# A hybrid convolution and attention block on one core: attention's copies, low parts and sums on separate products, two leading columns moved off GpSimd, attention steps placed anew

## The chip, the core and the metric

The kernel runs on one core of a Trainium2 chip. Its engines work side by side, each through its own queue in program order, and wait for one another by semaphores: TensorE (PE in the profile; PEld is its loading of weights), VectorE (DVE), ScalarE (ACT), GpSimd (POOL) and SyncE (SP). SP issues transfers only; POOL issues some of them between its own instructions. The metric is device time in microseconds (us). Before the change three runs took 2007.78, 2001.44 and 2006.52 us; their median is 2006.52 us.

## The reference, cut to what matters

One layer over 2048 positions of 1024 features, float32 throughout:

```python
h = rms_norm(x, norm_g)
v_c, b_c, c_c, z_c, q, k, v, z_a, gate_logits = jnp.split(jnp.einsum('bsd,dc->bsc', h, w_in), ...)
y_c = b_c * causal_depthwise_conv(c_c * v_c, conv_w)          # width 3: positions s-2, s-1, s
y_a = jnp.einsum('bsc,cd->bsd', y_c * silu(z_c), w_conv_out)
q = rms_norm(q per head, q_norm_g); k = rms_norm(k per head, k_norm_g)
o = sliding_window_attention(q, k, v, sinks) * silu(z_a)      # 16 heads of 64, 4 kv heads, window 128
y_b = jnp.einsum('bsc,cd->bsd', o, w_attn_out)
g_a, g_b = jnp.split(jax.nn.sigmoid(gate_logits + gate_b), 2, axis=-1)
x = x + jnp.einsum('bsd,de->bse', g_a * y_a + g_b * y_b, w_out)
```

Attention works on blocks of 128 positions, each against its own block and the one before it, with one learned sink per head in the softmax's sum.

## The kernel before, in words

**Tiles and units.** The sequence is done in two tiles of 1024 positions (t = 0, 1), and each tile in two halves of 512. A float32 operand is split into a high and a low part, and a matrix product is the sum of three (high by high, high by low, low by high). Every projection is cut into **units** of one weight group (`sunit`, from L424). A unit has seven products in the manner of Strassen's method, each of 12 matmuls of 128x512 (L412, in `product`), issued in the order 1, 5, 6, 2, 7, 3, 4. They land in three banks of PSUM: `X` takes products 1 and 2, `V` takes 5 and 3, `Y` takes 6, 7 and 4. Between them the side engines do the sums. After product 1 ACT copies `X` into `Y` (L430). After 5 ACT copies `V` into a spare tile `s5` (L439). After 6 DVE adds `V = s5 + Y`; product 7 writes `Y`, so this sum has the length of one product (2) to be done in. After 7 DVE adds `Y + s5`. The finished four quarters go to the unit's own closing function (`fin`).

**Weights.** A unit's weights are loaded as float32, and their sums and splits are made by pieces, one piece per product and some units ahead: a high part on ACT (L308, tiles ending in `_ah`, `_sh`, `_th`, `_d`), a low part on DVE (`_al`, `_sl`, `_tl`). DVE's instructions all carry L213, the line of the helper that records them.

**The order of the work.** It is written out by hand. `run` (from L599) counts one **tick** per product: it emits the product with its closing sums, then the weights' high part, then the first function that was put on this tick, then the weights' low part, then the other functions of the tick. Emission order is each engine's queue order. A function is put on a tick by `put(n, f)`.

**Stages of a tile** (times of tile 0 and tile 1 are in the table below): keys, values and queries; then the convolution, four times the unit sequence cv, cv, b (21 ticks); then the gates ga and gb (8 units each 7 ticks); then za and z (the SiLU gates), the two output projections ya and yb (L1143), and after both tiles the last projection o.

**Attention** runs beside the convolution and the gates: 32 steps a tile, each for a head group j and a block b. A step is placed on a tick n, and its parts on ticks counted from n by constants (L57): its loads at n-5 and n+V_ (SP); scores at n (PE L923 and L927, then a mask, a maximum and four short instructions on DVE); exponentials at n+1 (ACT L949 and four of L952); division at n+2 (DVE, three instructions); the flip at n+F_ (a DVE transposition into `f`, then a POOL-issued transfer to memory, `fd<-f`, L972); the way back at n+B_ (four POOL-issued transfers `x<-fd`, L979); the turn at n+X_ (ACT `xh` L986 and `yp` L987, DVE's low part `xl = x - xh`, four masks on POOL at L996); the product with the values at n+O_ (PE L1013, into `po`); and the output at n+O_+1, which for each of two halves copies one part of `po` by ACT (L1024) and adds the other by DVE, then stores.

**The convolution's closing function** (`fin_cv`, from L1030) gathers u = c*v, with two leading columns ahead of it, and one tick after the last product calls `edge`: GpSimd fills the leading columns (L1048 in tile 0, zeros; L1050 in tile 1, from a small tile `halo`), in tile 0 it keeps the last two columns in `halo` (L1052), and ACT then makes the first tap of both halves (L1055). The two other taps follow on DVE, one half on each of the two next ticks.

Of the kernel before, what the change touches and what calls it, by code (L numbers as in the profile page):

```python
# [19 lines left out]
H = 512  # L20
# [33 lines left out]
PE_TURNS = ((0, 0), (0, 1))  # L54
TURN_WAIT = 3

V_, F_, B_, X_, O_ = 6, 2, 5, 9, 13  # L57
HALVES = (LH, UH)


# [1 line left out]
def block_kernel(  # L62
# [12 lines left out]
    nc = tc.nc  # L75
# [18 lines left out]
    def slot(shape, dt, name):  # L94
        return big.tile(shape, dt, tag="big", name=name)
# [123 lines left out]
    vec = Woven()  # L219
# [383 lines left out]
    def run(gen):  # L603
        while True:
            tick[0] += 1
            if next(gen, gen) is gen:
                tick[0] -= 1
                return
            ahead_loads()
            hi, lo = (piece() if tick[0] >= W_FROM else None) or (None, None)  # L610
            if hi:
                hi()

            fs = at.pop(tick[0], [])
            for f in fs[:1]:
                f()
            if lo:
                lo()
            for f in fs[1:]:
                f()  # L620
            vec.some(WOVEN)

# [359 lines left out]
    def att_turn(t, j, b, pt):  # L982
        nm = f"{t}_{j}_{b}"
        xh, xl = slot([P, G, P], F32R, f"xh{nm}"), slot([P, G, P], F32R, f"xl{nm}")
        y = slot([P, G, P], F32R, f"yp{nm}")
        nc.scalar.copy(xh, pt)  # L986
        nc.scalar.copy(y[LH], pt[UH])  # L987
        vec.tensor_tensor(out=xl, in0=pt, in1=xh.bitcast(F32), op=ALU.subtract)

        def keep(dst, src, prev):
            sg = 1 if prev else -1
            d4 = dst.rearrange("p (e s) (g q) -> p e s g q", s=2, q=32)
            s4 = src.rearrange("p (e s) (g q) -> p e s g q", s=2, q=32)
            nc.gpsimd.affine_select(  # L996
                out=d4, in_=s4, pattern=[[0, 2], [-32 * sg, 2], [0, G], [-sg, 32]],
                compare_op=ALU.is_gt if prev else ALU.is_ge, fill=0.0, base=0,
                channel_multiplier=sg)

        keep(xh[UH], xh[UH], False)
        keep(y[LH], y[LH], True)
        keep(y[UH], xl[UH], True)
        keep(xl[UH], xl[UH], False)
        return xh, xl, y
# [12 lines left out]
    def att_out(t, j, b, po):  # L1018
        pov = po.rearrange("p (h e s c q) -> p h e s c q", h=2, e=2, s=2, c=2)
        o = slot([P, 2, P], F32, f"o{t}_{j}_{b}")  # L1020
        for e in range(2):
            own, oth = HALVES[e], HALVES[1 - e]
            ov = o[own].rearrange("p c (h s q) -> p h s c q", h=2, s=2)
            nc.scalar.copy(ov, pov[oth, :, e])  # L1024
            add(ov, pov[own, :, e], ov)
        nc.sync.dma_start(
            od[t][2 * j : 2 * j + 2, :, b * P : (b + 1) * P].rearrange("c p q -> p c q"), o)


    def fin_cv(t, k, ys):  # L1030
        u = upool.tile([P, 2 * H + 2], F32, tag="u", name=f"u{t}_{k}")
        halves = [u[:, 2 : 2 + H], u[:, 2 + H :]]
        hold = {}

        def fin(i, q, val):
            if (i, q) == (0, 0):
                nc.scalar.copy(halves[0], val)
            elif (i, q) == (1, 1):
                hold["v"] = plain(val, f"vr{t}_{k}")
            elif (i, q) == (0, 1):  # L1040
                mul(halves[1], val, hold["v"])
            else:
                mul(halves[0], val, halves[0])
                put(tick[0] + 1, edge)

        def edge():
            if t == 0:
                nc.gpsimd.memset(u[:, 0:2], 0.0)  # L1048
            else:
                nc.gpsimd.tensor_copy(u[:, 0:2], halo[:, k, :])  # L1050
            if t + 1 < NT:
                nc.gpsimd.tensor_copy(halo[:, k, :], u[:, 2 * H :])  # L1052
            for h in range(2):
                y = ys[k, h] = slot([P, H], F32, f"y{t}_{k}_{h}")
                nc.scalar.activation(out=y, in_=u[:, h * H : h * H + H], func=AF.Copy, scale=tap(0, k))  # L1055
            put(tick[0] + 1, lambda: taps(0))
            put(tick[0] + 2, lambda: taps(1))

        def taps(h):
            y = ys[k, h]  # L1060
            for i in (1, 2):
                vec.scalar_tensor_tensor(
                    out=y, in0=u[:, h * H + i : h * H + i + H], scalar=tap(i, k), in1=y,
                    op0=ALU.mult, op1=ALU.add)

        return fin
# [411 lines left out]
    def attention(t, places):  # L1478
        for r, n in enumerate(places):
# [13 lines left out]
            put(n + F_, step("f", lambda g, j=j, b=b: att_flip(t, j, b, g["n"])))  # L1493
            put(n + B_, step("b", lambda g, j=j, b=b: att_back(t, j, b, g["f"])))
            put(n + X_, step("x", lambda g, j=j, b=b: att_turn(t, j, b, g["b"])))
            put(n + O_, step("o", lambda g, j=j, b=b: att_values(t, j, b, g["x"], g["v"])))
            put(n + O_ + 1, step("z", lambda g, j=j, b=b: att_out(t, j, b, g["o"])))

    def next_tile(t, n0):

# [53 lines left out]
    for t in range(NT):  # L1554
# [3 lines left out]
        if t == 0:  # L1558
            t0 += 1

        attention(t, [t0 + 48 + 21 * (r // 4) + (0, 6, 10, 15)[r % 4] for r in range(16)] + [
            t0 + 129 + int(3.75 * r) for r in range(16)])
        if t > 0:
            run(sunit(("k", t), ops, fin_k(t)))
            run(sunit(("v", t), ops, fin_v(t)))
# [111 lines left out]
```

## Time and profile before

The profiled execution took 2005.35 us, of which the profile's span is 2003.6 us. Stages by their stretch of the span:

| stage | stretch, us | length, us | PE busy, us |
|---|---|---|---|
| keys, values, queries, tile 0 | 0 to 150 | 150 | 140.79 |
| convolution, tile 0, with attention | 150 to 400 | 250 | 246.59 |
| gates, tile 0, with attention | 400 to 600 | 200 | 192.62 |
| za, z, ya, yb of tile 0; k, v, q of tile 1 | 600 to 1045 | 445 | 443.99 |
| convolution, tile 1, with attention | 1045 to 1320 | 275 | 257.06 |
| gates and first za units, tile 1, with attention | 1320 to 1566 | 246 | 238.13 |
| the rest | 1566 to 2003.6 | 437.6 | 433.03 |

A row of the windows by stage reads: stretch and length, then for PE, PEld, DVE, ACT and POOL the busy time with the number of instructions, then the clock granted to TensorE (1.00 is full), the share of the transfer engines and GB/s. A row of the timeline reads: start, duration, engine, line, operation, what it writes and reads, and in brackets how long the engine had been idle before it and which instruction ended that. A row of the waits reads: the waiting instruction, what released it, then the total in us, how often, and the longest. A row of the groups by form reads: line, engine, operation, tiles, shape and count, then busy time in us and the mean of one in ns, then idle time ahead of the group and what ended it.

### The profile page before, as it was taken

What the parts mean: (1) busy time and instruction counts of PE and PEld (TensorE: products, weight loads), DVE (VectorE), ACT (ScalarE), POOL (GpSimd) and SP (SyncE); (2) the same over time, 40 slices, a digit from 0 to 9 for tenths busy, and PEclk for the clock granted to TensorE, in tenths of its full rate; (3) what the DMA queues carried; (4) which work ended last, traced back from release to release, by engine and by line L of the source; (5) the groups of instructions that cost most, each with busy time, mean ns of one, the idle gap of its engine ahead of it and who ended that gap; (6) DMA issues with size and microseconds to landing.
All of it is one profiled execution on the core that took longest, in us unless ns stands there. A gap on an engine that the chain in (4) does not pass through costs nothing.

```text
span 2003.6 us, 27366 instructions
## 1 busy us (share of the span) xinstructions
PE 1952.2 (97%) x8846; PEld 1607.5 (80%) x8846; DVE 1447.8 (72%) x2492; ACT 931.7 (47%) x1862; POOL 556.3 (28%) x850
## 2 busy tenths in 40 slices
PE   9999999999999999999999998899999999999999
PEld 7778877877788888888878787778878788888887
DVE  7989888887876564388798778778777556356654
ACT  7655455555664342235465444456565434222321
POOL 1472344354452000200562332335445000100000
PEclk9999999999999999999999999999999999999999
DMA  8485555566776435863674544567777434865553
GB/s 297 108 225 156 160 159 160 169 212 193 220 229 216 163 106 178 315 232 116 186 186 149 163 141 138 143 173 227 219 235 224 157 122 154 264 202 173 163 173 110
DMA packets 217374, 366.53 MB, mean 183 GB/s; under 512 B 29264, under 2 KB 104016, under 8 KB 217232
## 3 DMA queue, kind: packets, MB, share of 16 engines
q1 hardware_dynamic: 189696, 288.96, 45.8%
q0 software_dynamic: 27392, 75.80, 13.4%
q8 instruction: 70, 1.15, 0.2%
q14 instruction: 72, 0.59, 0.1%
q10 hardware_dynamic: 144, 0.03, 0.0%
HBM read 251.17 MB, written 113.51 MB: 182 GB/s over the span
## 4 chain that ended last, share of the span: by engine, by line
PE 53%; DVE 21%; DMA 8%; issue 6%; ACT 6%; POOL 3%; SPq 1%; DVEq 0%; POOLq 0%; ACTq 0%
PE Y L412 16%; PE yb L1143 9%; PE ya L1143 8%; DVE st L213 2%; PE Vo L412 2%; PE Xo L412 2%; PE Xz L412 2%; PE Vza L412 2%; PE Vz L412 2%; ACT p L952 2%; PE Xza L412 2%; DVE y L213 2%; DVE wcv_raw L213 1%; DMA x<-fd 1%; PE Xga L412 1%
## 5 line engine op out<-in xcount | busy, mean ns | idle before, releaser
L979 POOL DMA_DIRECT2D x<-fd x256 | 140.1, 554 | 47.7 <-DMA fd<-f 23.6
L996 POOL TENSOR_SCALAR_AFFINE_SELECT xh<-xh 64x512 fp32r<-64x512 f32 x64 | 63.0, 985 | 261.2 <-DVE xl L213 169.3
L952 ACT ACTIVATE p<-s,st,rq 128x128 f32<-128x128 f32 x256 | 112.8, 450 | 0.2 <-DMA lows<-kd 0.2
L972 POOL DMA_DIRECT2D fd<-f x64 | 37.0, 578 | 252.0 <-DVE f L213 181.1
L213 DVE TENSOR_TENSOR o<-po,o 64x256 f32<-64x256 f32 x128 | 53.2, 415 | 57.7 <-ACT o L1024 57.4
L213 DVE SCALAR_TENSOR_TENSOR tha<-tha,ya 128x512 f32<-128x512 f32 x32 | 22.0, 688 | 96.1 <-PE ya L1143 93.3
L1024 ACT COPY o<-po 64x256 f32<-64x256 f32 x128 | 46.9, 367 | 83.2 <-DVE o L213 81.1
L1143 PE MATMUL ya<-opa,wya_1h 128*128 128x512 f32 x256 | 79.5, 391 | 0.9 <-ACT opa L240 0.5
L412 PE MATMUL Xcv<-oph,wcv_ah 128*128 128x512 f32 x256 | 79.4, 391 | 0.0
L1143 PE MATMUL yb<-opb,wyb_1h 128*128 128x512 f32 x256 | 78.9, 389 | 0.0
L1143 PE MATMUL yb<-opb,wyb_0h 128*128 128x512 f32 x256 | 78.9, 389 | 0.0
L1143 PE MATMUL ya<-opa,wya_0h 128*128 128x512 f32 x256 | 78.8, 389 | 0.0
L240 ACT CAST opb<-ocr 128x512 fp32r<-128x512 f32 x32 | 19.9, 621 | 112.8 <-DMA ocr<-ocd 111.3
L213 DVE TENSOR_TENSOR xl<-x,xh 128x512 fp32r<-128x512 f32 x64 | 43.9, 687 | 35.4 <-ACT xh L986 30.0
L213 DVE SCALAR_TENSOR_TENSOR y<-u,cols,y 128x512 f32<-128x512 f32 x64 | 51.6, 807 | 20.1 <-ACT y L1055 17.4
L1231 POOL DMA_DIRECT2D wo<-in_w_out x16 | 8.7, 543 | 194.1 <-DVE opb L213 179.8
L521 POOL DMA_DIRECT2D x<-in_x x8 | 4.3, 540 | 201.4 <-PE ya L1143 200.6
L412 PE MATMUL Y<-oph,wcv_th 128*128 128x512 f32 x128 | 45.5, 440 | 13.2 <-DVE Vcv L213 13.2
L1143 PEld LDWEIGHTS ya<-opa,wya_1h 128*128 128x128 f32 x256 | 48.0, 188 | 12.2 <-ACT opa L240 1.3
L1143 PEld LDWEIGHTS ya<-opa,wya_0h 128*128 128x128 f32 x256 | 48.0, 188 | 10.0
L1143 PEld LDWEIGHTS yb<-opb,wyb_0h 128*128 128x128 f32 x256 | 48.0, 188 | 9.9
L1143 PEld LDWEIGHTS yb<-opb,wyb_1h 128*128 128x128 f32 x256 | 48.0, 188 | 9.9
(591 smaller groups left out, 6379.5 us busy)
## 6 DMA issues: line engine op xcount, KB each, us to landing
wcv_raw<-in_w_in SPq DMA_DIRECT2D x32, 512.0 KB, 4.1
q<-q2d SPq DMA_DIRECT2D x64, 256.0 KB, 4.7
fd<-f POOLq DMA_DIRECT2D x64, 256.0 KB, 4.0
x<-fd POOLq DMA_DIRECT2D x256, 64.0 KB, 3.8
v<-vd SPq DMA_DIRECT2D x128, 128.0 KB, 4.1
gd<-th SPq DMA_DIRECT2D x64, 256.0 KB, 2.8
wq_raw<-in_w_in SPq DMA_DIRECT2D x16, 512.0 KB, 5.2
q2d<-q_h POOLq DMA_DIRECT2D x64, 128.0 KB, 4.8
```

Source lines behind the costliest of these rows:

```text
L213: r = f(*args, **kw)
L240: nc.scalar.copy(hi, src)
L412: nc.tensor.matmul(ps, lhsT=w[:, j, :], rhs=b[:, m, :], start=start and j == 0 and i == 0, stop=j == KP - 1 and i == 2, skip_group_check=n ...
L521: eng.dma_start(xt, x2[r0 : r0 + P, :])
L952: nc.scalar.activation(out=p[:, i, :], in_=sg[:, i, HD : 3 * HD], func=AF.Exp, bias=st[:, 1, i : i + 1], scale=rv[:, i // 2, i % 2 : i % 2 ...
L972: nc.gpsimd.dma_start(fd, f)
L979: nc.gpsimd.dma_start(x[QUADS[k]], src[k])
L996: nc.gpsimd.affine_select(out=d4, in_=s4, pattern=[[0, 2], [-32 * sg, 2], [0, G], [-sg, 32]], compare_op=ALU.is_gt if prev else ALU.is_ge, ...
L1024: nc.scalar.copy(ov, pov[oth, :, e])
L1143: nc.tensor.matmul(ps, lhsT=w[:, j, cs], rhs=o[:, m, :], start=n == 0 and i == 0, stop=n == KC - 1 and i == 2)
L1231: nc.gpsimd.dma_start(h, w_o[c * P : (c + 1) * P, hs(q)])
```

## The change

Five edits.

1. The constants of an attention step: its value load moves from n+6 to n+4, the way back from n+5 to n+4; the flip, the turn and the product with the values keep theirs (2, 9, 13).
2. The turn at n+9 keeps only ACT's two copies; the low part on DVE and the four masks on POOL become a function of their own at n+10.
3. The output at n+14 keeps only ACT's two copies; the two sums on DVE and the store come at n+15.
4. The leading columns: zeros by DVE, the copies from and to `halo` by ACT.
5. The steps' ticks: the first 16 of a tile go three ticks later; of the second 16 the first goes three ticks later and the spacing is 3.5 instead of 3.75. And in `run` up to three functions of a tick, not one, are emitted ahead of the weights' low part.

```diff
-V_, F_, B_, X_, O_ = 6, 2, 5, 9, 13
+V_, F_, B_, X_, L_, O_, S_ = 4, 2, 4, 9, 10, 13, 15
...
             fs = at.pop(tick[0], [])
-            for f in fs[:1]:
+            for f in fs[:3]:
                 f()
             if lo:
                 lo()
-            for f in fs[1:]:
+            for f in fs[3:]:
                 f()
...
         nc.scalar.copy(xh, pt)
         nc.scalar.copy(y[LH], pt[UH])
+        return pt, xh, xl, y
+
+    def att_low(got):
+        pt, xh, xl, y = got
         vec.tensor_tensor(out=xl, in0=pt, in1=xh.bitcast(F32), op=ALU.subtract)
...
+        parts = []
         for e in range(2):
...
             nc.scalar.copy(ov, pov[oth, :, e])
-            add(ov, pov[own, :, e], ov)
+            parts.append((ov, pov[own, :, e]))
+        return o, parts
+
+    def att_sum(t, j, b, got):
+        o, parts = got
+        for ov, pv in parts:
+            add(ov, pv, ov)
         nc.sync.dma_start(
...
             if t == 0:
-                nc.gpsimd.memset(u[:, 0:2], 0.0)
+                vec.memset(u[:, 0:2], 0.0)
             else:
-                nc.gpsimd.tensor_copy(u[:, 0:2], halo[:, k, :])
+                nc.scalar.copy(u[:, 0:2], halo[:, k, :])
             if t + 1 < NT:
-                nc.gpsimd.tensor_copy(halo[:, k, :], u[:, 2 * H :])
+                nc.scalar.copy(halo[:, k, :], u[:, 2 * H :])
...
             put(n + X_, step("x", lambda g, j=j, b=b: att_turn(t, j, b, g["b"])))
-            put(n + O_, step("o", lambda g, j=j, b=b: att_values(t, j, b, g["x"], g["v"])))
+            put(n + L_, step("w", lambda g: att_low(g["x"])))
+            put(n + O_, step("o", lambda g, j=j, b=b: att_values(t, j, b, g["w"], g["v"])))
             put(n + O_ + 1, step("z", lambda g, j=j, b=b: att_out(t, j, b, g["o"])))
+            put(n + S_, step("t", lambda g, j=j, b=b: att_sum(t, j, b, g["z"])))
...
-        attention(t, [t0 + 48 + 21 * (r // 4) + (0, 6, 10, 15)[r % 4] for r in range(16)] + [
-            t0 + 129 + int(3.75 * r) for r in range(16)])
+        attention(t, [t0 + 51 + 21 * (r // 4) + (0, 6, 10, 15)[r % 4] for r in range(16)] + [
+            t0 + 132 + int(3.5 * r) for r in range(16)])
```

DVE's queue has 2494 instructions before and 2502 after, ACT's 1593 and 1607, POOL's 855 and 831; PE's 8848 and SP's 1266 stay.

What this does to the queues is shown at three places, all in the convolution of tile 1, about the unit of weights `wcv_3`, whose profiled products before lie near 1140 us. A name such as `o_0_2` is head group 0, block 2, with a buffer number behind it; `s_0_4` are the scores of step 4. The next unit's weights, `wb_1`, are being made in the third.

DVE, before, the last rows up to the unit's sum `Vcv_3` (the mask and maximum of `s_0_4` stand some rows further up):

```order
L213 TENSOR_TENSOR st_0_4_10733<-st_0_4_10733 128x4
L213 RECIPROCAL st_0_4_10733<-st_0_4_10733 128x4
L213 TENSOR_TENSOR p_0_4_10755<-p_0_4_10755,st_0_4_10733 128x512
L213 STREAM_TRANSPOSE f_0_4_10798<-p_0_4_10755 128x512
L213 TENSOR_TENSOR o_0_2_10822<-po_0_2_10788,o_0_2_10822 64x4x2x32 x2
L213 TENSOR_TENSOR xl_0_3_10829<-x_0_3_10697,xh_0_3_10828 128x512
L213 SCALAR_TENSOR_TENSOR y_2_0_10803<-u_2_10568,cols,y_2_0_10803 128x512 x2
L213 TENSOR_TENSOR Vcv_3_10807<-s5cv_3_10820,Y 128x512
```

and DVE of the change at the same sum:

```order
L213 TENSOR_TENSOR xl_0_2_10718<-x_0_2_10574,xh_0_2_10717 128x512
L213 TENSOR_TENSOR o_0_1_10750<-po_0_1_10710,o_0_1_10750 64x4x2x32 x2
L213 COPY_PREDICATED s_0_4_10781<-mask_i,s_0_4_10781 128x4x64
L213 TENSOR_REDUCE st_0_4_10789<-s_0_4_10781 128x4
L213 TENSOR_TENSOR st_0_4_10789<-st_0_4_10789,rq_0_9609 128x4
L213 SCALAR_TENSOR_TENSOR st_0_4_10789<-st_0_4_10789,nsink_r 128x4
L213 TENSOR_TENSOR st_0_4_10789<-cols,st_0_4_10789 128x4
L213 SCALAR_TENSOR_TENSOR y_2_0_10759<-u_2_10527,cols,y_2_0_10759 128x512 x2
L213 TENSOR_TENSOR Vcv_3_10763<-s5cv_3_10776,Y 128x512
```

Step 4's division and flip, which stood ahead of `Vcv_3`, now follow it; its mask and maximum have come down to just ahead of it. The output sums and the low part ahead of it are those of steps 1 and 2, where they were of steps 2 and 3.

ACT, before, at the same products:

```order
L430 COPY Y<-Xcv_3_10770 128x512
L1055 ACTIVATE y_2_0_10803<-u_2_10568,cols 128x512
L1055 ACTIVATE y_2_1_10805<-u_2_10568,cols 128x512
L439 COPY s5cv_3_10820<-Vcv_3_10807 128x512
L1024 COPY o_0_2_10822<-po_0_2_10788 64x4x2x32 x2
L986 CAST xh_0_3_10828<-x_0_3_10697 128x512
L987 CAST yp_0_3_10830<-x_0_3_10697 64x512
```

and ACT of the change:

```order
L986 CAST xh_0_2_10717<-x_0_2_10574 128x512
L987 CAST yp_0_2_10719<-x_0_2_10574 64x512
L430 COPY Y<-Xcv_3_10732 128x512
L1029 COPY o_0_1_10750<-po_0_1_10710 64x4x2x32 x2
L1061 COPY u_2_10527<-halo 128x2
L1066 ACTIVATE y_2_0_10759<-u_2_10527,cols 128x512
L1066 ACTIVATE y_2_1_10761<-u_2_10527,cols 128x512
L439 COPY s5cv_3_10776<-Vcv_3_10763 128x512
L308 CAST wb_1_ah<-wb_1_raw_10542 128x1024
```

The copy from `halo` now stands in ACT's own queue just ahead of the tap that reads it, and no copy of `po` or `x` stands between `s5cv_3` and the weights' next part.

DVE, before, around the low part `wb_1_sl` of the next unit, four products on:

```order
L213 TENSOR_TENSOR wb_1_raw_10585<-wb_1_raw_10585,wb_1_raw_10583 128x512
L213 TENSOR_TENSOR st_0_5_10915<-st_0_5_10915,rq_0_9609 128x4
L213 TENSOR_TENSOR wb_1_raw_10583<-wb_1_raw_10583,wb_1_raw_10585 128x512
L213 SCALAR_TENSOR_TENSOR st_0_5_10915<-st_0_5_10915,nsink_r 128x4
L213 TENSOR_TENSOR st_0_5_10915<-cols,st_0_5_10915 128x4
L213 TENSOR_TENSOR u_3_10769<-Vcv_3_10807,vr_3_10900 128x512
L213 TENSOR_TENSOR wb_1_sl<-wb_1_raw_10585,wb_1_sh 128x1024
```

and of the change:

```order
L213 TENSOR_TENSOR wb_1_raw_10544<-wb_1_raw_10544,wb_1_raw_10542 128x512
L213 TENSOR_TENSOR wb_1_raw_10542<-wb_1_raw_10542,wb_1_raw_10544 128x512
L213 TENSOR_TENSOR u_3_10731<-Vcv_3_10763,vr_3_10871 128x512
L213 TENSOR_TENSOR o_0_2_10873<-po_0_2_10844,o_0_2_10873 64x4x2x32 x2
L213 TENSOR_TENSOR xl_0_3_10877<-x_0_3_10726,xh_0_3_10876 128x512
L213 TENSOR_TENSOR wb_1_sl<-wb_1_raw_10544,wb_1_sh 128x1024
```

Two output sums and an attention low part now stand ahead of the weights' low part (before, the output sums of this tick came behind it), and the mask and maximum of step 5 no longer do.

## The prediction

> **What bounds the kernel now.** The page's first part:
>
> ```profile
> span 2003.6 us, 27366 instructions
> PE 1952.2 (97%) x8846; PEld 1607.5 (80%) x8846; DVE 1447.8 (72%) x2492; ACT 931.7 (47%) x1862; POOL 556.3 (28%) x850
> ```
>
> TensorE bounds it. The change leaves PE's instructions as they are, so it can win only what PE loses: idle time (2003.6 - 1952.2 = 51.4 us), and busy time run at a lower clock. The windows by stage show where this lies; quoted are the four stages with attention, which alone the change touches:
>
> ```profile
> 150.00:400.00 250.00, 246.59 (x1145) 202.79 (x1144) 213.97 (x389) 126.39 (x290) 90.56 (x143) 1.00 0.55 161
> 400.00:600.00 200.00, 192.62 (x909) 159.56 (x909) 155.63 (x288) 120.96 (x293) 100.86 (x145) 0.99 0.72 213
> 1045.00:1320.00 275.00, 257.06 (x1157) 210.70 (x1156) 221.51 (x394) 129.28 (x296) 92.08 (x140) 0.97 0.50 147
> 1320.00:1566.00 246.00, 238.13 (x1116) 197.00 (x1116) 187.35 (x330) 147.88 (x338) 115.54 (x166) 0.99 0.72 218
> ```
>
> Idle PE: 3.41 (convolution, tile 0), 7.38 (gates, tile 0), 17.94 (convolution, tile 1) and 7.87 us (gates, tile 1), together 36.6. For the clock I cut windows out of these:
>
> ```profile
> 409.40:412.80 3.40, 3.40 (x9) 2.67 (x8) 3.33 (x6) 0.38 (x1) 0.58 (x1) 0.50 0.87 213
> 1145.10:1150.00 4.90, 4.90 (x12) 3.88 (x13) 3.97 (x4) 0.00 (x0) 3.83 (x6) 0.50 0.56 165
> 1218.40:1221.70 3.30, 3.30 (x9) 2.53 (x8) 3.26 (x4) 0.00 (x0) 3.23 (x6) 0.50 0.57 174
> 1290.70:1296.80 6.10, 6.10 (x16) 4.94 (x17) 4.56 (x5) 0.00 (x0) 3.84 (x6) 0.50 0.47 136
> 1557.30:1563.00 5.70, 5.70 (x17) 4.73 (x18) 2.85 (x4) 1.82 (x4) 0.00 (x0) 0.50 0.47 141
> ```
>
> In these 23.4 us PE runs at half the full clock, which costs half of them: 1.7 + 7.15 (the three of tile 1's convolution) + 2.85 = 11.7 us. So 48.3 us is all that can be won. What PE waits for, in PE's waits:
>
> ```profile
> PE Y L412 <- DVE Vcv L213: 13.2, 7, 3.8
> PE Y L412 <- DVE th L213: 4.5, 4, 1.7
> PE s L923 <- ACT p L952: 3.6, 3, 2.1
> PE Vza L412 <- DVE wza_sl L213: 2.2, 1, 2.2
> ```
>
> The first row is the sum after product 6, which DVE brings late. The timeline ahead of one of its three long stalls, all engines:
>
> ```profile
> 1137.23 0.58 POOL L972 DMA_DIRECT2D fd<-f  x1 [7.58 <-DVE f L213]
> 1137.86 0.18 POOL L1050 COPY u<-halo 128x2 f32<-128x2 f32 x1
> 1138.08 1.34 ACT L1055 ACTIVATE y<-u,cols 128x512 f32<-128x512 f32 x2 [2.60 <-POOL u L1050]
> 1139.32 0.56 ACT L439 COPY s5cv<-Vcv 128x512 f32<-128x512 f32 x1
> 1140.31 0.42 DVE L213 TENSOR_TENSOR o<-po,o 64x256 f32<-64x256 f32 x1 [3.37 <-ACT o L1024]
> 1140.76 0.36 ACT L1024 COPY o<-po 64x256 f32<-64x256 f32 x1 [0.48 <-DVE o L213]
> 1141.16 0.43 DVE L213 TENSOR_TENSOR o<-po,o 64x256 f32<-64x256 f32 x1 [0.43 <-ACT o L1024]
> 1141.80 0.69 DVE L213 TENSOR_TENSOR xl<-x,xh 128x512 fp32r<-128x512 f32 x1 [0.21 <-ACT xh L986]
> 1142.41 1.90 DVE L213 SCALAR_TENSOR_TENSOR y<-u,cols,y 128x512 f32<-128x512 f32 x2
> 1144.34 0.70 DVE L213 TENSOR_TENSOR Vcv<-s5cv,Y 128x512 f32<-128x512 f32 x1
> 1145.09 1.22 PE L412 MATMUL Y<-oph,wcv_th 128*128 128x512 f32 x2 [3.82 <-DVE Vcv L213]
> ```
>
> Read it upward. PE waits for `Vcv`, queued behind the taps, `xl` and the `o` sums. DVE stood idle 3.37 + 0.43 + 0.21 = 4.01 us waiting for ACT; ACT stood 2.60 us for POOL's two columns; POOL had held these behind a transfer issue that waited for DVE's flip. A full circle of four engines: DVE, POOL, ACT, DVE. DVE's idle time alone, 4.01, exceeds PE's stall of 3.82.
>
> **The change part by part.** *Leading columns.* In tile 1 the `halo` copy moves into ACT's queue just ahead of the tap. POOL's wait no longer reaches ACT. Prices, from the groups by form:
>
> ```profile
> L1055 ACT ACTIVATE y<-u,cols 128x512 f32<-128x512 f32 x32 | 21.4, 717 | 43.5 <-POOL u L1050 29.6 <-POOL u L1048 13.9
> L1048 POOL MEMSET u<- 128x2 f32 x8 | 0.8, 102 | 0.3
> L721 ACT COPY q_g<-qss 32x32 f32<-32x32 f32 x24 | 5.2, 218 | 0.6
> L213 DVE TENSOR_TENSOR st<-st,rq 128x4 f32<-128x4 f32 x64 | 16.1, 252 | 1.9
> ```
>
> ACT's waits for these columns (29.6 + 13.9 us) end. It gains 16 copies; no such copy stands on ACT in this trace, so between nothing and 0.22 us each (its smallest copies, L721), I take 0.22: 3.5 us, on an engine that is 47% busy. DVE gains eight zeros of two columns: between 0.10 (the same on POOL) and 0.25 us (DVE on four columns), I take 0.25, 2 us in tile 0. ACT's tap there now waits for DVE's queue instead of POOL's; the old wait was 13.9 / 8 = 1.7 us each and tile 0 bore it, so I put this at nothing, and at up to 1.7 us for each of eight units, 14 us, if DVE is behind. That end goes into the range.
>
> *Copies, low part and sums apart.*
>
> ```profile
> L213 DVE TENSOR_TENSOR o<-po,o 64x256 f32<-64x256 f32 x128 | 53.2, 415 | 57.7 <-ACT o L1024 57.4
> L1024 ACT COPY o<-po 64x256 f32<-64x256 f32 x128 | 46.9, 367 | 83.2 <-DVE o L213 81.1
> L213 DVE TENSOR_TENSOR xl<-x,xh 128x512 fp32r<-128x512 f32 x64 | 43.9, 687 | 35.4 <-ACT xh L986 30.0
> L996 POOL TENSOR_SCALAR_AFFINE_SELECT xh<-xh 64x512 fp32r<-64x512 f32 x64 | 63.0, 985 | 261.2 <-DVE xl L213 169.3
> ```
>
> ACT's two copies, 0.37 each, get a product (2.7 us) to finish before DVE adds, and `xh` as long before DVE subtracts. DVE is freed of up to 57.4 + 30.0 = 87.4 us of standing, ACT of 81.1. The amount of work is the same. The store and the masks come a product later. The four masks of a step at about 1 us each (L996; it is the first and the dearest of them) have three products, 8.2 us, before the values read them: nothing. If POOL comes to them more than 4 us late, PE waits for the rest. POOL still stands for flips (7.58 us above), but only attention's masks queue behind that now. The store's only readers are the za units, much later.
>
> *Earlier way back (n+4).* The transfers' row, its last number the us to landing:
>
> ```profile
> fd<-f POOLq DMA_DIRECT2D x64, 256.0 KB, 4.0
> ```
>
> The way back issues four transfers on POOL one product sooner; if `fd<-f` has not landed, POOL waits, and masks behind it too. The flip is two products, 5.4 us, ahead, so I take nothing. A DVE that is late with the flip makes POOL stand for as long, at most the product by which the step was moved, 2.7 us, inside the masks' 4 us of cover. `xh` gets five products instead of four after it. That matters at the end of the steps:
>
> ```profile
> 1548.94 0.62 ACT L986 CAST xh<-x 128x512 fp32r<-128x512 f32 x1 [5.95 <-DMA x<-fd]
> 1554.31 0.73 PE L412 MATMUL Vza<-oph,wza_sh 128*128 128x512 f32 x2 [0.83 <-ACT wza_sh L308]
> 1557.27 0.79 PE L412 MATMUL Vza<-oph,wza_sl 128*128 128x512 f32 x1 [2.23 <-DVE wza_sl L213]
> ```
>
> ACT stood 5.95 us for a late `x`; the weights' parts behind it came late, and PE lost 0.83 + 2.23 us and the half clock that follows. The new lead of 2.7 us covers a half of the 5.95; the rest I count as covered too, since with the new spacing and the masks at n+10 a step's transfers no longer share a tick with another step's masks on POOL. If that is wrong, 0.83 + 2.23 + 2.85 = 5.9 us stay. The value load two products earlier is one more early entry in SP's queue of loads; nothing here waits for it, so nothing.
>
> *New ticks and three functions ahead of the low parts.* The ticks take step 4's division and flip from ahead of `Vcv` to behind it: two DVE operations of 128x512, at the 0.69 of `xl` about 1.4 us, an estimate. Against that, up to 2 x 0.415 + 0.687 = 1.52 us stands ahead of a `_sl`. I walked DVE's queue in the new order with the durations above: with no standing, `_sl` comes with about a microsecond to spare in most units and with none in one unit of each convolution period of tile 1.
>
> *The sum.* The same 302 matmuls of three units take, in tile 0 and in tile 1:
>
> ```profile
> 213.44:278.88 65.44, 64.36 (x302) 53.11 (x302) 54.88 (x95) 33.15 (x76) 25.76 (x40) 1.00 0.54 160
> 1150.40:1222.70 72.30, 66.34 (x302) 54.23 (x301) 56.52 (x94) 32.95 (x76) 25.48 (x38) 0.98 0.50 145
> ```
>
> Tile 1's convolution loses 17.94 + 7.15 = 25.1 us. Brought to tile 0's rate it gains 72.30 - 65.44 = 6.9 at each of three long stalls: 20.6. The gates lose 7.38 + 1.7 = 9.1 and 7.87 + 2.85 = 10.7 us; brought to tile 0's convolution (3.41 idle in 250 us, so 2.7 and 3.4 left) they gain 6.4 and 7.3. Tile 0's convolution: nothing. Together 34.3 us off 2005.35: 1971.0. The median of the runs is 1.2 above the profiled execution, so **1972**.
>
> **The clock, by row and by rule.** Half clock followed the gaps of 3.8 us, but also the 0.83 + 2.23 above and, at 409 us, the wait for `p` of 2.1 (PE's waits, third row). The Trainium skill, TensorE: Matmul & The Clock Gate, section "HAM oscillation — how this bites in real kernels", gives the rule "no PE-idle gaps >~3.4µs". By it the stretches at 409 and 1557 us have another cause than those gaps and may stay, and the sum is rival E's time instead of the forecast's. The trace speaks against it: both stretches come right behind gaps of 2.1 and 2.23 us, and none stands elsewhere.
>
> **Rivals.**
> *A, only the POOL wait goes.* The three long stalls shrink by ACT's 2.60 us each and lose their half clock: 7.8 + 7.15 = 15 us, **1990**. For it: `Vcv` remains behind taps, sums and `xl` (0.70 + 1.90 + 0.69 + 0.83 us) in one queue. Against: the 4.01 us of standing in that queue also ends.
> *B, all goes:* 2005.35 - 48.3 = 1957, with the median **1958**. For it: nothing in my walk stands still for long. Against: tile 0, without the POOL circle in its way, still loses 3.41.
> *C, slower: the weights' low parts come late.* 1.52 us of attention stands ahead of `_sl`. Twelve units a convolution and sixteen a pair of gates make 56 in both tiles; a loss of 1.52 in more than 34.3 / 1.52 = 23 of them undoes the gain, and in 30 of them the time is 2006.5 - 34.3 + 45.6 = **2018**. It decides if DVE has no slack. Against: in tile 0's period DVE is busy 54.88 of 65.44 us.
> *D, nothing moves:* DVE's standing is only handed to the next instruction in the queue, and the stalls appear elsewhere: **2005**. Against: the circle needs POOL.
> *E, half clock stays at 409 and 1557 us* whatever the gaps: 1.7 + 2.85 less gain, **1976.5**. Against: both stretches directly follow gaps.
>
> **Chances.** Forecast 0.53, A 0.16, B 0.14, E 0.05, C 0.07, D 0.05. So faster by over 0.3% (6 us, about what a measurement of this kernel can tell from no change) 0.88, within 0.3% 0.05, slower 0.07. The range holds B, the forecast, E and A with a part of the tap's 14 us: 1956 to 1996.
>
> **What would show it.** Right: in tile 1's convolution the row "PE Y <- DVE Vcv" falls from 13.2 us to under 3; "DVE o <- ACT o", "DVE xl <- ACT xh" and "ACT y <- POOL" fall from 57.4, 30.0 and 43.5 to a few us; tile 1's period takes 65 to 67 us; the clock windows near 1145, 1218 and 1290 are gone. Wrong: a `_sl` row among PE's waits above 10 us (C), `Vcv` stalls of over 1 us left in each period (A), or ACT's tap waiting for DVE's zeros in tile 0 with PE idle there above 6 us.

## The result, and the profile after

The changed kernel took 1948.51 us (median of four runs, 1946.77 to 1949.01) against 2005.06 us of four runs of the kernel before (2001.44 to 2007.78): 0.9718 of it, 95% interval 0.9699 to 0.9736. It is faster, as forecast, but by more than the range allowed: 1972 was predicted, with 1956 as the lower end. The profiled execution took 1946.77 us with a span of 1945.1 us; the comparison of the traces is between the spans, 2003.6 and 1945.1, 58.5 us apart.

The page's first part, of the kernel after:

```profile
span 1945.1 us, 27476 instructions
PE 1928.7 (99%) x8846; PEld 1601.9 (82%) x8846; DVE 1460.0 (75%) x2500; ACT 937.9 (48%) x1876; POOL 581.5 (30%) x826
```

TensorE's idle time fell from 51.4 to 16.4 us and its busy time, with the same 8846 matmuls, by 23.5 us. Of that busy time, 11.9 us were the cost of half clock. The windows by stage of the kernel after, cut at the same projection matmuls as the four stages shown of before (attention's steps come later against these cuts, so 12 of its matmuls pass from tile 0's convolution to the gates behind it, and 6 in tile 1):

```profile
150.10:391.40 241.30, 241.30 (x1133) 202.33 (x1132) 215.48 (x390) 126.18 (x294) 93.34 (x126) 1.00 0.53 164
391.40:581.10 189.70, 189.70 (x922) 160.24 (x921) 159.77 (x297) 126.75 (x304) 110.68 (x149) 1.00 0.79 236
1026.30:1273.90 247.60, 246.41 (x1151) 205.55 (x1150) 214.56 (x385) 129.81 (x295) 90.52 (x124) 1.00 0.52 159
1273.90:1507.60 233.70, 233.36 (x1123) 196.52 (x1122) 201.33 (x340) 149.70 (x346) 126.91 (x174) 1.00 0.76 234
```

The stages took 250.0, 200.0, 275.0 and 246.0 us before: they gained 8.7, 10.3, 27.4 and 12.3 us, 58.7 together, which is all of it. By what such matmuls take elsewhere in the trace, about 1.5 us of the first figure and 0.7 of the third are attention's matmuls that the gates took over. Idle time is 0, 0, 1.19 and 0.34 us, and the clock stands at 1.00 in all four. DVE, 87% busy in tile 1's convolution, works without PE having to wait. The three units that took 65.44 us in tile 0 and 72.30 us in tile 1, and PE's longest waits:

```profile
211.50:275.00 63.50, 63.50 (x302) 53.35 (x301) 56.37 (x97) 33.55 (x78) 26.73 (x36) 1.00 0.53 166
1123.40:1187.60 64.20, 63.87 (x302) 53.32 (x301) 55.01 (x95) 33.50 (x78) 27.01 (x37) 1.00 0.53 164
```

```profile
PE Vcv L412 <- DVE wcv_sl L213: 2.8, 4, 1.6
PE Vq L412 <- ACT q_t L505: 2.0, 1, 2.0
PE ptr L536 <- DVE rtok L530: 1.6, 1, 1.6
```

The waits for `Vcv`, `th`, `p` and `wza_sl` shown of before are gone; what leads now belongs to the start of the program, which the change leaves alone, but for three waits of 0.34 us for `_sl` in tile 1. The place of the long stall, in the timeline of after (rows of ACT, DVE and PE in order of time; the same convolution unit, 24 us earlier):

```profile
1111.29 0.68 DVE L213 TENSOR_TENSOR xl<-x,xh 128x512 fp32r<-128x512 f32 x1
...
1111.74 0.75 ACT L1029 COPY o<-po 64x256 f32<-64x256 f32 x2
...
1112.51 0.19 ACT L1061 COPY u<-halo 128x2 f32<-128x2 f32 x1
1112.52 0.85 DVE L213 TENSOR_TENSOR o<-po,o 64x256 f32<-64x256 f32 x2 [0.55 <-ACT o L1029]
1112.74 1.34 ACT L1066 ACTIVATE y<-u,cols 128x512 f32<-128x512 f32 x2
...
1113.98 0.56 ACT L439 COPY s5cv<-Vcv 128x512 f32<-128x512 f32 x1
...
1116.30 1.54 DVE L213 SCALAR_TENSOR_TENSOR y<-u,cols,y 128x512 f32<-128x512 f32 x2
```

```profile
1117.76 0.69 DVE L213 TENSOR_TENSOR Vcv<-s5cv,Y 128x512 f32<-128x512 f32 x1
```

```profile
1120.67 0.63 PE L412 MATMUL Y<-oph,wcv_th 128*128 128x512 f32 x2
```

ACT copies `po` and the two columns and goes on without a bracket; DVE stands 0.55 us where it stood 4.01; `Vcv` ends at 1118.45, 2.2 us before PE asks for it. The groups by form that answer to those of before:

```profile
L213 DVE TENSOR_TENSOR o<-po,o 64x256 f32<-64x256 f32 x128 | 53.4, 418 | 2.2 <-ACT o L1029 1.1
L1029 ACT COPY o<-po 64x256 f32<-64x256 f32 x128 | 47.1, 368 | 2.3
L213 DVE TENSOR_TENSOR xl<-x,xh 128x512 fp32r<-128x512 f32 x64 | 43.4, 679 | 0.8
L1066 ACT ACTIVATE y<-u,cols 128x512 f32<-128x512 f32 x32 | 21.5, 720 | 2.4 <-DVE u L213 2.2
L1061 ACT COPY u<-halo 128x2 f32<-128x2 f32 x8 | 1.6, 194 | 0.1
L213 DVE MEMSET u<- 128x2 f32 x8 | 0.5, 60 | 0.0
```

### The profile page after: what moved, and what is told of

It reads as the page before. It is cut to its first block, busy times and chain, and to the rows that moved or that the text cites. A ratio compares the mean times of both kernels' runs of the same rounds, so it can differ in the third digit from the quotient of the medians.

```text
span 1945.1 us, 27476 instructions
## 1 busy us (share of the span) xinstructions
PE 1928.7 (99%) x8846; PEld 1601.9 (82%) x8846; DVE 1460.0 (75%) x2500; ACT 937.9 (48%) x1876; POOL 581.5 (30%) x826
## 4 chain that ended last, share of the span: by engine, by line
PE 84%; DVE 8%; DMA 3%; issue 2%; POOL 2%; ACT 1%; SPq 0%; DVEq 0%; POOLq 0%; ACTq 0%
PE Y L412 26%; PE yb L1154 9%; PE ya L1154 8%; PE Vcv L412 4%; PE Xcv L412 4%; PE Xgb L412 2%; PE Vgb L412 2%; PE Xza L412 2%; PE Vza L412 2%; PE Vga L412 2%; PE Xz L412 2%; PE Vo L412 2%; PE Xo L412 2%; PE po L1017 2%; PE Xga L412 2%
## 5 line engine op out<-in xcount | busy, mean ns | idle before, releaser
L1000 POOL TENSOR_SCALAR_AFFINE_SELECT xh<-xh 64x512 fp32r<-64x512 f32 x64 | 73.4, 1147 | 140.8 <-DVE xl L213 119.6
L1000 POOL TENSOR_SCALAR_AFFINE_SELECT xl<-xl 64x512 fp32r<-64x512 f32 x64 | 67.9, 1062 | 4.4
L1000 POOL TENSOR_SCALAR_AFFINE_SELECT yp<-yp 64x512 fp32r<-64x512 f32 x64 | 56.9, 889 | 4.2
L1154 PEld LDWEIGHTS ya<-opa,wya_1h 128*128 128x128 f32 x256 | 48.0, 188 | 12.3 <-ACT opa L240 1.3
L774 POOL DMA_DIRECT2D q2d<-q_h x64 | 44.2, 691 | 41.2 <-ACT q_t L505 18.8
L1000 POOL TENSOR_SCALAR_AFFINE_SELECT yp<-xl 64x512 fp32r<-64x512 f32 x64 | 55.2, 863 | 3.1
L308 ACT CAST wcv_sh<-wcv_raw 128x1024 fp32r<-128x1024 f32 x16 | 16.8, 1053 | 80.5 <-DVE wcv_raw L213 80.5
```

The lines of the kernel that those rows point to most:

```text
L308: return (lambda: nc.scalar.copy(hi, src), lambda: vec.tensor_tensor(out=lo, in0=src, in1=hi.bitcast(F32), op=ALU.subtract))
L774: nc.gpsimd.dma_start(q2d[t][j][half, q * 2 * HB : (q + 1) * 2 * HB, i, e, :], src[HALVES[e]].bitcast(F32).rearrange("p (b x) -> p b x", x ...
L1000: nc.gpsimd.affine_select(out=d4, in_=s4, pattern=[[0, 2], [-32 * sg, 2], [0, G], [-sg, 32]], compare_op=ALU.is_gt if prev else ALU.is_ge, ...
L1154: nc.tensor.matmul(ps, lhsT=w[:, j, cs], rhs=o[:, m, :], start=n == 0 and i == 0, stop=n == KC - 1 and i == 2)
```

## The experiments

Two theories were set against each other. **Circle**: the stalls come from engines standing for one another (POOL for DVE's flip, ACT for POOL's columns, DVE for ACT's copies), and each link taken out shortens them. **Queue**: the sums are late because of what stands ahead of them in DVE's own queue, so the new ticks decide. Kernels of one group of runs share the runs of the kernel before.

| kernel | us | before beside it | ratio, 95% interval |
|---|---|---|---|
| before + leading columns | 1983.54 | 2003.93 | 0.9894 (0.9876 to 0.9911) |
| before + low part and sums apart | 1972.31 | 2003.93 | 0.9838 (0.9818 to 0.9858) |
| before + both | 1960.54 | 2003.93 | 0.9781 (0.9764 to 0.9798) |
| before + apart + new ticks | 1960.94 | 2003.93 | 0.9783 (0.9766 to 0.9800) |
| the change, columns on GpSimd | 1952.61 | 2001.60 | 0.9752 (0.9732 to 0.9772) |
| the change, old V_ and B_ | 1950.30 | 2001.60 | 0.9742 (0.9719 to 0.9765) |
| the change, one function ahead | 1950.93 | 2001.60 | 0.9744 (0.9725 to 0.9764) |
| the change, all old ticks | 1965.38 | 2001.60 | 0.9818 (0.9798 to 0.9838) |
| the change, first sixteen old ticks | 1964.25 | 2004.53 | 0.9795 (0.9778 to 0.9812) |
| the change, low part and sums not apart | 1985.18 | 2004.53 | 0.9902 (0.9881 to 0.9922) |
| the change + known stalls | 2009.53 | 2004.53 | 1.0022 (1.0012 to 1.0032) |

**The leading columns alone.**

```diff
-                nc.gpsimd.memset(u[:, 0:2], 0.0)
+                vec.memset(u[:, 0:2], 0.0)
             else:
-                nc.gpsimd.tensor_copy(u[:, 0:2], halo[:, k, :])
+                nc.scalar.copy(u[:, 0:2], halo[:, k, :])
             if t + 1 < NT:
-                nc.gpsimd.tensor_copy(halo[:, k, :], u[:, 2 * H :])
+                nc.scalar.copy(halo[:, k, :], u[:, 2 * H :])
```

> The kernel before with the leading columns on DVE and ACT, nothing else of the change. Circle theory (the long stalls of tile 1's convolution come from the circle POOL, ACT, DVE, and every link taken out shortens them): the three stalls of 3.8 us lose ACT's 2.60 us of waiting for POOL and their half clock, 7.8 + 7.15 = 15 us, so about 1990 us against 2005. Queue theory (the sum after product 6 is late because of what stands ahead of it in DVE's own queue, whoever waits): the stalls stay over 3 us, 2003 to 2006.

It took 1983.54 us, 20.4 less than before. PE's waits, and one of the three stalls:

```profile
PE Y L412 <- DVE Vcv L213: 5.1, 5, 1.4
PE Y L412 <- DVE th L213: 4.2, 3, 2.2
```

```profile
1137.63 0.73 PE L412 MATMUL Y<-oph,wcv_th 128*128 128x512 f32 x2 [1.39 <-DVE Vcv L213]
```

Each of the three fell from 3.8 to between 1.33 and 1.39 us, that is by 2.4, close to the 2.60 that ACT had stood for POOL, and no half clock is left in tile 1's convolution. The queue theory, 2003 to 2006, falls; the circle's mechanism holds, and its 15 us was short by 5. The waits in the gates (`th`), where no columns exist, stay.

**Low part and sums apart, alone.** The constants are `V_, F_, B_, X_, L_, O_, S_ = 6, 2, 5, 9, 10, 13, 15`; ticks, columns and the one function ahead are those of before.

```diff
-            add(ov, pov[own, :, e], ov)
+            parts.append((ov, pov[own, :, e]))
...
+            put(n + L_, step("w", lambda g: att_low(g["x"])))
...
+            put(n + S_, step("t", lambda g, j=j, b=b: att_sum(t, j, b, g["z"])))
```

> The kernel before with the low part and the output sums one product behind ACT's copies (n+10, n+15), old ticks, old leading columns, one function ahead of the low parts. Circle theory: DVE no longer stands 3.37 + 0.43 + 0.21 us for ACT's copies, but ACT's tap is still 2.60 us late, so the stalls come down to about 1 us and lose their half clock: 3 x 2.8 + 7 = 15 us, about 1990. Queue theory: 2003 to 2006, since the sums and the low part still stand somewhere ahead of a sum after product 6.

1972.31 us, 31.6 less: twice the circle's 15. The waits of PE, and ACT's for the columns:

```profile
PE po L1017 <- POOL xl L1000: 9.1, 10, 1.3
PE Y L412 <- DVE Vb L213: 2.4, 3, 1.2
```

```profile
ACT y L1066 <- POOL u L1059: 19.1, 7, 5.2
ACT y L1066 <- POOL u L1061: 16.6, 8, 3.8
```

The long waits for `Vcv` are gone from tile 1 although ACT's tap still stood 35.7 us for POOL, and so are those of the gates (`th`, `wza_sl`), where no columns exist: the handing to and fro between ACT's copies and DVE's sums was the cost there too (this run does not tell DVE's standing from ACT's). In their place PE now waits for the masks on POOL, which come a product later.

**Both, old ticks.** The two diffs above together.

> Both together, old ticks. Circle theory: tile 1's convolution falls to the rate of tile 0's (65.5 us for three units, from 72.3), the gates stay: 2005 - 21 = 1984. Queue theory: above 1995, with stalls of over 1 us left at the sum after product 6.

1960.54 us against 1984 expected. The forecast for tile 1's convolution was right in direction (no PE wait of 0.25 us or more is left there but one of 0.54 at its first unit), but the gates had been counted as unmoved and had gained with the sums. The two edits alone give 20.4 and 31.6 us, together 43.4 and not 52.0: each alone shortens the same stalls. What is left above the change is mostly masks:

```profile
PE po L1017 <- POOL xl L1000: 6.1, 7, 1.3
```

**Apart, new ticks, three functions ahead; old columns, old V_ and B_.**

```diff
-            for f in fs[:1]:
+            for f in fs[:3]:
...
-        attention(t, [t0 + 48 + 21 * (r // 4) + (0, 6, 10, 15)[r % 4] for r in range(16)] + [
-            t0 + 129 + int(3.75 * r) for r in range(16)])
+        attention(t, [t0 + 51 + 21 * (r // 4) + (0, 6, 10, 15)[r % 4] for r in range(16)] + [
+            t0 + 132 + int(3.5 * r) for r in range(16)])
```

> The new ticks, three functions ahead of the low parts, and the low part and sums apart, but the leading columns still on GpSimd and the old offsets of the value load and the way back. Circle theory: the flips that POOL waits for still hold the columns up, so tile 1's convolution keeps stalls of about 2 us in each of three periods: 1960 to 1970. Queue theory: as good as the whole change, 1947 to 1952, because the flip then stands behind the sum and the columns have time.

1960.94 us: at the circle's lower end. Tile 0's convolution and its gates have no waits over 0.25 us; tile 1's convolution keeps, in three periods, a wait of 0.4 us for the masks, one of 0.8 us for `b` and one of 1.2 to 1.3 us for the taps `y`, some 2.5 us a period. That is near the 2 us expected, but hardly any of it (0.1 to 0.2 us) is at `Vcv`. The queue theory's 1947 to 1952 misses by 9.

**Back from the change: the columns on GpSimd.** The first diff reversed.

> The changed kernel with the leading columns back on GpSimd. Circle theory: what the run with new ticks and old columns lost in tile 1's convolution (waits of 1.2 us for the tap y and 0.8 us for the sum b in three periods, at 1960.9 us) comes from GpSimd's two columns, so this is as slow, 1959 to 1962. Offset theory (the way back at n+4 is what took those waits away): near the whole change, 1948 to 1951.

**Back from the change: V_ and B_.**

```diff
-V_, F_, B_, X_, L_, O_, S_ = 4, 2, 4, 9, 10, 13, 15
+V_, F_, B_, X_, L_, O_, S_ = 6, 2, 5, 9, 10, 13, 15
```

> The changed kernel with the value load at n+6 and the way back at n+5, as before the change. Circle theory: these two offsets do nothing, 1948 to 1950. Offset theory: they carry the 12 us between the run with new ticks and old columns and the whole change, 1957 to 1961.

1952.61 and 1950.30 us. The first is near the offset theory's number, the second is the circle's: neither theory holds alone. With columns and offsets old the ratio was 0.9783, with only the columns old 0.9752, with only the offsets old 0.9742, with neither 0.9718. The two edits cover one another: either alone already removes most of the 12 us that both missing cost. The columns on GpSimd still make ACT stand,

```profile
ACT y L1066 <- POOL u L1061: 22.8, 6, 4.5
ACT y L1066 <- POOL u L1059: 7.0, 4, 2.2
```

some 30 us of it, but with the way back a product earlier (and the value load two, which no run takes apart from it) PE has no wait over 0.34 us behind that convolution's first unit. So the link that the prediction made so much of is worth 20 us on the kernel before and 4 on the changed one. The intervals of these two runs and of the change overlap, and the differences of 2 to 4 us are not settled: in the profile with the columns on GpSimd, 1.7 us are the cost of a stretch at half clock near 83 us, ahead of attention and the convolution.

**One function ahead of the low parts.** `fs[:3]` back to `fs[:1]`.

> The changed kernel with one function of a tick ahead of the weights' low part, as before. If the order in a tick matters little: 1947 to 1950. If up to 1.5 us of attention ahead of a low part is what leaves PE waiting for it (0.3 to 0.5 us at 1030, 1155, 1219 and 1283 us, with some 0.27 us beside each): 1946 to 1947. If attention needs the place ahead of the low part: above 1953, with waits for attention's tiles.

1950.93 us, its interval overlapping with the change's. The three waits of 0.34 us for `_sl` in tile 1 are still there, so it isn't the functions ahead of the low part that cause them. PE waits 1.7 us for masks that it did not wait for in the change. Its profile also has two stretches at half clock, which cost 3.4 us, at 8 and 83 us, ahead of attention and the convolution.

**All old ticks, and only the first sixteen.**

> The changed kernel with the old ticks for the attention steps. If the ticks carry the last 12 us (the run with columns, low part and sums moved but old ticks took 1960.5, with PE waiting 0.4 to 1.3 us for masks on GpSimd in tile 0's convolution): 1958 to 1962, with the same waits. If the way back at n+4 or the three functions ahead of the low parts carry them: 1948 to 1952.

```diff
-        attention(t, [t0 + 51 + 21 * (r // 4) + (0, 6, 10, 15)[r % 4] for r in range(16)] + [
+        attention(t, [t0 + 48 + 21 * (r // 4) + (0, 6, 10, 15)[r % 4] for r in range(16)] + [
```

> The changed kernel with the old ticks for the first sixteen steps of each tile alone (three earlier); the second sixteen stay at the new ticks and spacing. With all old ticks it took 1965.4 us; its waits lay in tile 0's convolution and just behind it (0.5 to 1.5 us for masks on GpSimd, 0.7 for the sum after product 6). If those come from the first sixteen's places: 1960 to 1965. If they come from the spacing 3.75 of the second sixteen: 1949 to 1952.

1965.38 us with all old ticks, 1964.25 us with those of the first sixteen steps alone: the three ticks' shift in the convolution carries what the ticks are worth, some 16 us (with all old ticks 1958 to 1962 was expected), and the spacing of the second sixteen has no part that these runs can tell. With the first sixteen old, PE's shown waits are 11.6 us longer than in the change: 8.0 of it is for the masks, in tile 0's convolution and just behind it, and 2.2 for the sum `Vb`. Two views of the run with the first sixteen old, POOL's masks and PE's wait:

```profile
211.54 1.68 POOL L1000 TENSOR_SCALAR_AFFINE_SELECT xh<-xh 64x512 fp32r<-64x512 f32 x1 [8.32 <-DVE xl L213]
213.29 0.74 POOL L1000 TENSOR_SCALAR_AFFINE_SELECT yp<-yp 64x512 fp32r<-64x512 f32 x1
214.08 1.08 POOL L1000 TENSOR_SCALAR_AFFINE_SELECT yp<-xl 64x512 fp32r<-64x512 f32 x1
215.22 1.81 POOL L1000 TENSOR_SCALAR_AFFINE_SELECT xl<-xl 64x512 fp32r<-64x512 f32 x1
```

```profile
217.09 0.38 PE L1017 MATMUL po<-xl,v 128*128 128x256 f32 x1 [1.50 <-POOL xl L1000]
```

and the masks of the change at its corresponding step:

```profile
213.40 0.76 POOL L1000 TENSOR_SCALAR_AFFINE_SELECT xh<-xh 64x512 fp32r<-64x512 f32 x1 [4.13 <-DVE xl L213]
214.22 0.74 POOL L1000 TENSOR_SCALAR_AFFINE_SELECT yp<-yp 64x512 fp32r<-64x512 f32 x1
215.00 0.73 POOL L1000 TENSOR_SCALAR_AFFINE_SELECT yp<-xl 64x512 fp32r<-64x512 f32 x1
215.81 0.76 POOL L1000 TENSOR_SCALAR_AFFINE_SELECT xl<-xl 64x512 fp32r<-64x512 f32 x1
```

With the old ticks POOL got `xl` from DVE only 3.5 us before PE began with `po` (215.06 us), and its four masks took 5.5 us, since one of the same form ran now 0.75, now 1.7 or 1.8 us. In the change they took 3.2 us and were done 3 us before PE came (219.64 us).

**Low part and sums not apart.** The change with the low part and the masks at n+9 and each sum right behind its copy at n+14.

> The changed kernel with the low part and masks back on the product of ACT's copies (n+9) and the output sums between the copies (n+14). This alone won most on the kernel before (1972.3 of 2003.9 us). If it is needed whatever the ticks: 1965 to 1980, with PE waiting for the sum after product 6. If the new ticks and the moved columns already give DVE the time: 1950 to 1955.

1985.18 us, above the 1965 to 1980 expected: of the edits undone this costs most, 37 us, more than the 31.6 that it won alone. PE's waits:

```profile
PE s L923 <- ACT p L952: 6.3, 6, 1.1
PE Y L412 <- DVE Vgb L213: 5.2, 8, 0.9
PE Y L412 <- DVE zas L213: 3.7, 2, 1.9
```

Some 26 us of shown idle time, in 30 waits of about 1 us spread over both tiles' gates and tile 0's convolution; no half clock, and tile 1's convolution stays free. So the new ticks do not pay without the sums apart.

**Known stalls.** The changed kernel with the sum after product 6 done again 3 to 9 times in 17 units of za, z and o, where it has no waits of its own.

```diff
         product(Y, u, 6, ops, False)
         add(vb, s5, Y)
+        for _ in range(LATE.get(nm, 0)):
+            nc.vector.tensor_tensor(out=vb, in0=s5, in1=Y, op=ALU.add)
```

> The changed kernel with known stalls put where it has none: in 17 units of za, z and o the sum after product 6 is done 3 to 9 times more (it reads s5 and Y and writes V, so doing it again changes nothing), each time 0.62 to 0.7 us. By the changed kernel's times (sum at 679.76 us, the next product at 682.22) three repeats make PE wait some 0.15 us, four 0.8, five 1.4, six 2.0, seven 2.6, eight 3.3, nine 3.9; 33.7 us over all units. Theory of the cost: of each such wait the profile shows 0.27 us less as idle time, since the last matmul before and the first after are drawn longer; so the shown idle time falls short of the longer span by 17 x 0.27 = 4.6 us, half clock aside. Rival: the 11.6 us that the change won beyond idle time and half clock come from other engines' traffic, and here the span grows by the shown idle time and half clock alone. Theory of the clock: it is judged in fixed stretches of 3.413 us, and a stretch with over about 1.9 us of shown idle time is followed by one at half clock; so waits under 1.9 us bring none, and of the eight waits of 1.9 us or more four to seven do, by where the stretch ends. Rival by the Trainium skill's rule of gaps over 3.4 us: one or none does.

PE's waits, and one of them:

```profile
PE Y L413 <- DVE Vz L445: 25.8, 8, 4.6
PE Y L413 <- DVE Vo L445: 13.0, 6, 4.0
PE Y L413 <- DVE Vza L445: 2.9, 2, 1.8
```

```profile
672.52 0.73 PE L413 MATMUL Y<-oph,wz_th 128*128 128x512 f32 x2 [2.52 <-DVE Vz L445]
```

A repeat took 0.73 us, so the waits were longer than planned (1.06, 1.79, 2.52, 3.25, 3.95 us for four to eight repeats). *The cost.* The profiled span is 65.7 us longer than the change's. Shown idle time accounts for 40.1 (52.3 against 12.2), the half clock for 21.3 (44.4 us of it, less the idle time inside, halved). The rest, 4.3 us over 16 visible waits, is 0.27 each; 4.6 was expected. The rival, no rest at all, falls. In the rows of such a wait at full clock the last matmul before it is followed 0.16 us later than its like and the first one after by 0.11 us, which is 0.27 again and the firmer measure: that the sum agrees so well is in part chance. Matmul by matmul, the matmuls of its first 11 us are 2.2 us longer than in the change, two pairs of short waits at `ya` are missing (1.1 us less), and half clock cost nearer 20 us than 21.3.

*The clock.* Half clock came in stretches that start on a grid of 3.413 us. All ten waits of 2.5 us and more were followed by one, and one of the three of 1.79 us. Windows of two of these three, one grid stretch and the next:

```profile
645.80:649.21 3.41, 1.62 (x8) 1.04 (x7) 3.27 (x6) 1.10 (x2) 0.00 (x0) 1.00 0.18 67
649.24:652.60 3.36, 3.36 (x9) 2.58 (x10) 1.50 (x2) 0.00 (x0) 0.00 (x0) 0.50 0.00 0
1574.20:1577.60 3.40, 2.48 (x11) 1.70 (x10) 3.26 (x5) 0.89 (x2) 0.00 (x0) 1.00 0.50 191
1577.60:1581.00 3.40, 2.54 (x11) 2.12 (x12) 2.50 (x4) 0.22 (x1) 0.00 (x0) 1.00 0.00 0
```

The first wait lies in one stretch (1.79 us of 3.41 idle) and the next runs at half clock; the second is as long, but cut in two by the grid (0.92 and 0.86), and nothing follows. Eleven against the expected four to seven, because the waits were longer; the rule of gaps over 3.4 us would have given four, those of 3.9 us and more; by the expectation's sizes it was one.

## Why the prediction was right or wrong, point by point

**What bounds it, and the circle: right.** The columns alone took 2.4 us out of each 3.8 us stall, and every sign named for the mechanism came: the row "Y <- DVE Vcv" is gone (under 3 us forecast), "DVE o <- ACT o" fell from 57.4 to 1.1 us, "DVE xl <- ACT xh" and "ACT y <- POOL" are gone, the windows at half clock too. Tile 1's period is 64.2 us, below the 65 to 67 given. Of the circle's links the one between ACT's copies and DVE's sums weighs more: with it gone and POOL's left, the long stalls went altogether, while the columns alone left 1.4 us of each.

**"So 48.3 us is all that can be won": wrong, the first failed step.** It took PE's shown idle time and half clock for the whole loss. Of the span's 58.5 us, shown idle time makes 35.0 (51.4 to 16.4), half clock 11.9, and 11.6 us are neither: with every wait the matmuls on either side of it are drawn longer and count as busy. The ruler measured 0.27 us a wait. The kernel before has 34 more waits over 0.06 us than the change, so 9.2 us of the 11.6 by this price. The traces bear it out: at full clock and behind the first 150 us, the matmuls beside shown waits are 8.8 us longer before than in the change, and in the seven other traces with ten or more additional waits they are longer by 0.26 to 0.31 us a wait. The last 2 us are of the same kind, at waits too short to be shown as idle: matmuls that have no shown wait beside them, but take over 0.04 us longer than their like, make 3.1 us of excess before and 0.7 after. Among them are the scores' matmuls (0.62 to 1.02 us a step before, 0.62 to 0.78 after).

**"Brought to tile 0's rate" and "tile 0's convolution: nothing": wrong, the second.** This left 4.5, 2.7, 3.4 and 3.4 us of loss in the four stages, 14.0 in all, though the walk through DVE's queue had found nothing standing for long. It left 1.5. Tile 0's convolution was no floor: it had 3.4 us of shown waits of its own, at the taps, `_sl` and the scores, its 970 projection matmuls took 3.6 us less with these gone, and it gained 8.7 us, some 1.5 of them attention's matmuls handed to the gates. These two steps are the whole miss: 34.3 forecast, 12.5 too much left over, 11.6 not seen, 58.4 us of 58.5.

**Rivals.** B, all goes, is what happened; at 0.14 it had too small a chance, and its 1957 was still 10 us above the 1946.77 of the profiled execution: the unseen 11.6, less the 1.5 that stayed. A is half right as a mechanism and was measured by itself: the POOL wait alone is worth 20.4 us, not 15. C: three waits of 0.34 us for `_sl`, in one unit of each period of tile 1, as the walk had one without slack there, and no more; the run with one function ahead shows that these functions are not their cause. E falls: both stretches at half clock went with the gaps ahead of them. D falls.

**Costs put at nothing.** The copies of the columns on ACT took 0.19 us each (0.22 taken), the zeros on DVE 0.06 (0.25 taken), and ACT's tap waits 2.2 us in all for DVE, so the 14 us of the range were not needed. The earlier way back (with the value load) is not nothing: it stands in for the columns' move when that is undone. The masks, "nothing" with 4 us of cover, are the one term that would have been dear: with the old ticks PE waited 7 us and more for them, and only the new ticks give the cover.

**The clock.** The prediction set the row (half clock after 2.1 and 2.23 us) against the Trainium skill's rule, TensorE: Matmul & The Clock Gate, section "HAM oscillation — how this bites in real kernels", of no gaps over 3.4 us. The rows were right, the rule of the gap's length was not. The same page's section "What's actually happening" has the activity judged in a window of 3413 ns that runs free of the kernel; the grid of 3.413 us found here agrees with that.

## What to carry to other kernels

Where two engines hand work to and fro inside one step (copy, add, copy, add), put the halves a step apart: the standing of either in its in-order queue is paid by whatever queues behind. Move such edits together and test them so, since each covers for the other: the columns' move was worth 20 us alone and 4 us beside the rest, and the spread of the sums gave its whole worth only with new ticks for the masks that it made later (1965.38 us with the old). And when idle time of the bounding engine is added up for a forecast, add about 0.27 us for each of its waits (measured here, between matmuls of 128x512), and look for half clock where idle time gathers within one 3.4 us stretch.

## What the runs showed of the hardware that was not expected

Half clock depends on where a wait falls. In the traces of the twelve other kernels a grid stretch of 3.413 us, at full clock, with a single wait in it was followed by half clock from 1.93 us of shown idle time on, and not up to 1.87; the ruler has one at 1.79. With two waits in the stretch 1.50 to 1.58 us was enough in three cases, and in a fourth, also of 1.50, it was not. Counted with 0.27 us a wait, these border cases lie between 2.0 and 2.2 us of 3.41, and there both outcomes are found. The wait of some 1.95 us near 82 us, at the start of the queries, is in nearly every kernel here. In five traces it fell into one stretch and half clock followed, in the others the grid cut it: the same wait costs 1.7 us more or not.

The masks on POOL, one form (64x512), took 0.73 to 1.77 us in the change, with DVE at work beside the longer ones for more of their time: 74 of 1.0 to 1.2 us had operations of DVE with two inputs and over 0.3 us beside them for 0.83 of their time, 137 under 0.85 us for 0.41. The 32 of over 1.6 us had 0.77, no more than those of 1.1, so this does not explain the longest. The Trainium skill, GPSIMD Engine Reference, section "1. Specifications", says that its access to the on-chip memory is shared with VectorE, with contention for operations of two inputs; the rows are in keeping with it, but no run took the operations away, so the cause is not shown.
